# An encoder layer in split fp32: the last pair's operand splits one embedding block later, sums of two output units made in memory, and two gate units' sums one product sooner

## The chip, the cores and the metric

The kernel runs on one core of one Trainium2 chip. The metric is the device time of one execution in microseconds (us). The kernel before takes 2235.86 us (median of 3 runs, 2234.56 to 2236.57).

## What is computed

One layer of a hybrid encoder on 512 tokens of width 2048, in fp32:

```
h   = rms_norm(x);  one projection h @ w_in gives
      group A: banded attention, 16 heads of 64 (own 64-token chunk + 8 before), with a bias
      group B: gated linear attention (GLA), 4 heads, per-head norm, times silu(gate)
x  += concat(group A, group B) @ w_out
x  += conv3-gated FFN of width 5632 (up, gelu, down)
x  += sigmoid(rms_norm(x) @ w_ple_gate) * (p @ w_ple_proj)      p: 512 x 256
out = rms_norm(x)
```

## The kernel before

**Products.** Every large matrix product is cut into *units*: a unit yields a 256-row block of the result in four quarters, and it does so by seven products P1 to P7 instead of eight, as in Winograd's form of Strassen's scheme. The weights' side of the seven is L11, L12, S2, S1, S3, S4 and L22, where S1 = L21+L22, S2 = S1+L11, S3 = L21+L11, S4 = S2+L12; each is a page of 128x1024 (512 KB). The other side is one of seven stored operands, R11, R21, R22, N1, N2, T3, T4, each in two halves of four k-blocks. A product runs in one of three accumulators, accA, accB, accC: P1 and P4 in A, P2 in B, and so on.

**Splits.** TensorE gets its precision from splitting each operand: ScalarE (ACT) writes the rounded high part (`wsplit<-l`, `wsplit<-s`, `wo_R<-...`), VectorE (DVE) subtracts it and writes the low part (`wsplit<-l,wsplit`). A product is 24 matmuls: high by high, high by low, low by high, over 8 k-blocks. An accumulator is collected by ACT if its quarter is new (`u<-accA`) and else added by DVE (`u<-u,accA`).

**Order.** A list `steps` gives one product a step; the first two and the last two units of a stage are interleaved, P1 of both, P2 of both, and so on. `agenda[step]` holds pairs (k, function): k = 0 before the step's weight split, 1 behind its high part, above 1 behind its product. In the main loop ACT, DVE and TensorE (PE) keep this program order (all their rows carry line 64, the helper that does that). The weight split stands two steps ahead of its product.

**Stages.** A value projection; `linear` (GLA heads 16 to 19, values 20 to 23, gate units 8 and 9, in the order 16, 20, 21, 17, 22, 23, 18, 8, 9, 19); `front` (attention units 0 to 7 and gate units 10, 11); then four *embedding blocks* (p @ w_ple_proj, `embedding`, L728), one step each; `wo` (eight units of w_out); the FFN; the last norm. Gate units 8 to 11 are g = 0 to 3. For g below 2, `times` (u = u·on, with `on` the GLA head read back from memory, L860) and `pair` (`store_pair`: three stores of u, four sums `tp` on DVE, four stores, SP's L264) are put behind the unit's products by the list at L872.

**An embedding block** is 24 matmuls of 128x512, `pp<-ps,wsplit`, in four banks of PSUM of its own, that is, four chunks of six. ACT evicts each chunk (`pp_o<-pp`); two chunks make a *pair*, which shares one page and is stored to memory from ACT's own DMA queue (`ppd<-pp_o`, L742). A block has two pairs. The eight pairs use the pages u2, u3, c2, u1, c1, c2, u1, c1, so from the sixth pair on ACT must see a store land before it may evict into the page again: the third block's second pair needs the store of the second block's first pair (c2); the fourth block's two pairs need the stores of the second block's second pair (u1) and of the third block's first pair (c1).

**The operands of wo** are loaded from memory, except the last two k-blocks of each second half (the *tails*): `tails[0]` is the last attention pair (`wo_R<-yp`) and `tails[1]` gate unit 11's u (`wo_R<-u`, sums `wo_N<-tp`, `wo_T<-tp`), which never go to memory. `wo.split(op, 1, False, (1,))` splits such a tail, at the agenda place that the last table of the diff gives. Gate unit 11's u is multiplied by `on` just before.

**Weight sums.** A page of the kind "dma" (`issue`, L390) is loaded with L21 by SP (L409) and L22 or L11 is added to it by an accumulating DMA of GpSimd (POOL, L410); S2 is added up by DVE in a page of its own, and S4 in place of S2 (`s<-s,l`). Wo's first and last two units are of that kind before. A page goes back into `free` when its last use is done, and the next wanted load is issued then.

**Transfers and semaphores.** Plain transfers, of SP and ACT alike, use eight semaphores in rotation, so each also waits for the eighth one before it in the program.

Of the kernel before, what the change touches and what calls it, by code (L numbers as in the profile page):

```python
# [8 lines left out]
F32 = mybir.dt.float32  # L9
# [3 lines left out]
ALU = mybir.AluOpType  # L13
# [30 lines left out]
def encoder_block(ctx: ExitStack, tc: tile.TileContext, A, out):  # L44
# [256 lines left out]

    class Stage:
        def __init__(self, name, units, kb, xd, weights, after, sums, edge, last=PLAIN, begin=None, begin_at=0,
                     chained=False, pace=None, late=(), single=False, groups=None):
            self.name, self.kb, self.xd, self.weights, self.after = name, kb, xd, weights, after
            self.begin, self.begin_at, self.pace, self.late = begin, begin_at, pace, late
            self.chained, self.tail, self.quarter = chained, [None, None], None
            self.n = (4, kb - 4 - 2 * chained)
            self.x = {}
            n = len(units)  # L310
            self.units = [Unit(self, u, last if i >= n - 2 else PLAIN, edge if i < 2 or i >= n - 2 else sums)
                          for i, u in enumerate(units)]
            for i in range(n):
                self.units[i].pos = i
            if single:
                self.groups = [[self.units[i] for i in g] for g in groups or [(i,) for i in range(n)]]
# [13 lines left out]
        def split(self, op, g, body=True, tails=(0, 1)):  # L330
# [6 lines left out]
            if self.chained and g == 1:  # L337
# [4 lines left out]


    NEEDS = {"own": ("L11", "L12", "S1", "S3", "L22"), "dma": ("L11", "L12", "S1", "S2*", "S3", "L22"), "dve": ("L11", "L12", "L21", "L22", "S1*", "S2*"),
             "s3": ("L11", "L12", "L21", "L22", "S1*", "S2*")}

    class Unit:
        def __init__(self, stage, u, order, sums):
            self.stage, self.u, self.order, self.sums = stage, u, order, sums
            self.first, self.head, self.last = False, None, None  # L350
            self.w, self.tag = {}, {}
            self.kind, self.lead = None, self
            if sums in ("own", "dma"):
                self.uses = dict(L11=2, L12=2, S1=2, S2=2, S3=1, L22=1)
                self.made = {"S2", "S4"}
            else:
                self.uses = dict(L11=3, L12=2, S1=2, S2=2, L21=2, L22=2)
                self.made = {"S1", "S2", "S3", "S4"}
            self.parts = dict(C11=2, C12=2, C22=2, C21=1)
            self.have = set()  # L360
            self.left = dict(A=4, B=1, C=2)
            self.o = None
            self.banks = {}

    free, wanted, retired = [], [], []

    def retire(tag):
        if tag in free:
# [21 lines left out]
    def issue():  # L390
        kept, i = 0, 0
        while i < len(wanted):
            unit, name = wanted[i]
            if len(free) <= kept:
                return
            if name[-1] == "*":
                kept += 1
                i += 1
                continue
            wanted.pop(i)  # L400
            n = unit.stage.kb * P
            t = raw_page(unit, name)[:, :n]
            src = lambda q: unit.stage.weights(unit.u, q)
            if name[0] == "L":
                d = nc.sync.dma_start(t, src(name))
                if unit.stage is stages[-1] and unit.last is not None:
                    tc.keep_in_program_order(d)
            else:
                nc.sync.dma_start(t, src("L21"))  # L409
                nc.gpsimd.dma_start(t, src("L22" if name == "S1" else "L11"), accum_op=ALU.add)  # L410
# [41 lines left out]
    def prep_high(i, own=None):  # L452
        if i >= len(steps):
            return None
        unit, prod = steps[i]
        name = PRODUCTS[prod][0]
        n = unit.stage.kb * P
        make(unit, name)
        if prod == unit.order[0] and unit.sums not in ("own", "dma"):
            make(unit, "S1")  # L460
        if i + 1 < len(steps):
            nxt, p = steps[i + 1]
            q = PRODUCTS[p][0]
            if (nxt is unit or nxt.paired) and (q != "S4" or "P6" in nxt.w):
                make(nxt, q)
        if i > 0 and steps[i - 1][1] == "P6" and steps[i - 1][0].paired:
            make(steps[i - 1][0], "S4")
        key = {"S4": "S2"}.get(name, "L21" if name == "S3" and unit.sums not in ("own", "dma") else name)
        raw = unit.w[key]
# [224 lines left out]
    def after_gate(unit):  # L694
# [7 lines left out]

    blk2 = lambda w: lambda m, q: w[m + 8 * (q[1] == "2"), int(q[2]) - 1]
    stages = [Stage("wo", list(range(8)), 8, mixd, blk2(A["w_out"]), after_norm(streams[1], h2d, nffn), "s3", "dma",
                    begin=lambda u: load_x(streams[0], u), begin_at=6, chained=True)]
    order, f0, slots = [], 0, {}
    for ci, n in enumerate(CHUNKS):
        for k in range(n // 2):
# [153 lines left out]
    def after_gates(unit):  # L862
        g, M = unit.u - 8, unit.M

        def times():
            vec.tensor_tensor(unit.o, unit.o, M["on"], ALU.mult)

        def pair():
            ops = store_pair(mixd if g < 3 else None, 3 + g, unit.o[:, 0, :], unit.o[:, 1, :])
            if g == 3:  # L870
                tails[1] = ops

        return [(0, 1, lambda: vec.tensor_tensor(unit.o, unit.o, rb2, ALU.mult)),
                (1 if g < 2 else 0, 1.5, lambda: act.activation(unit.o, unit.o, AF.Silu))] + (
                    [(4, 1, times), (5, 1, pair)] if g < 2 else [(1, 1, times), (1, 3, pair)] if g == 2 else
                    [(0, 3, times), (0, 4, pair)])

    gla = {}
# [262 lines left out]
    for n, p in enumerate(PLAIN):  # L1141
# [4 lines left out]
            agenda[i0 + (15 if kept else n + 5)].append((3, lambda op=op, g=g: wo.split(op, g, True, ())))  # L1146
        at = (7, 7, 8, 9, 15, 10, 11)[n]
        agenda[i0 + at].append((3.5, lambda op=op: wo.split(op, 1, False, (0,))))
        at, k = ((8, 1), (9, 1), (10, 1), (12, 1), (15, 3.6), (14, 3), (15, 3.6))[n]
        agenda[i0 + at].append((k, lambda op=op: wo.split(op, 1, False, (1,))))  # L1150

    def embedding_load(raw):
# [21 lines left out]
    def more_banks():  # L1174
        aux_tags[:] = ["b6", "b7"]
        banks.extend(("b4", "b5"))

    agenda[base[front.units[7]] + 7 + 12].append((5, attention_done))
    agenda[i0 + 11].append((0, more_banks))
# [356 lines left out]
```

## Time and profile before

| | before |
|---|---|
| median of 3 runs | 2235.86 us (2234.56 to 2236.57) |
| the profiled execution's own time | 2234.99 us |
| its span, first to last instruction | 2233.0 us |
| mean granted TensorE clock | 0.997 |
| busy: PE / DVE / ACT / POOL | 2192.7 / 1921.8 / 1339.0 / 158.3 us |
| PE's idle time in the span | 40.3 us |
| chain that ended last: PE / DVE / DMA / ACT | 83% / 8% / 3% / 3% |

All rows below come from the profiled execution. Its time is 1.99 us above its span and 0.87 us below the median. A row of a timeline has the start, the busy time, the engine, the line, the operation, out<-in, the tile, and in brackets the idle time of the engine just before, with what ended it. A "DMA" row of a chain or a bracket is a transfer from issue to landing. One row can stand for several like instructions in succession (x48). The times of places: gate units 8 and 9 end at 300 to 335 us, the embedding blocks run from 597 to 625, and wo's first products from 625 on.

### The profile page before, as it was taken

What the parts mean: (1) busy time and instruction counts of PE and PEld (TensorE: products, weight loads), DVE (VectorE), ACT (ScalarE), POOL (GpSimd) and SP (SyncE); (2) the same over time, 40 slices, a digit from 0 to 9 for tenths busy, and PEclk for the clock granted to TensorE, in tenths of its full rate; (3) what the DMA queues carried; (4) which work ended last, traced back from release to release, by engine and by line L of the source; (5) the groups of instructions that cost most, each with busy time, mean ns of one, the idle gap of its engine ahead of it and who ended that gap; (6) DMA issues with size and microseconds to landing.
All of it is one profiled execution on the core that took longest, in us unless ns stands there. A gap on an engine that the chain in (4) does not pass through costs nothing.

```text
span 2233.0 us, 46278 instructions
## 1 busy us (share of the span) xinstructions
PE 2192.7 (98%) x18588; PEld 2143.9 (96%) x18588; DVE 1921.8 (86%) x2632; ACT 1339.0 (60%) x2005; POOL 158.3 (7%) x196
## 2 busy tenths in 40 slices
PE   9999999999999999999999999999999999999997
PEld 8899999999899989999999999999999999999996
DVE  8476778999879888999888898989898797998988
ACT  9455565777665665555555555555564554666765
POOL 0000000000000100000000000000000100001000
PEclk9999999999999999999999999999999999999998
DMA  7466875667888988888888888888876967879996
GB/s 237 138 183 187 224 204 157 179 187 197 286 253 271 325 237 208 215 230 216 224 218 222 216 224 218 211 223 208 254 235 231 315 231 247 313 252 322 296 288 201
DMA packets 190761, 518.31 MB, mean 232 GB/s; under 512 B 20273, under 2 KB 66609, under 8 KB 190545
## 3 DMA queue, kind: packets, MB, share of 16 engines
q1 hardware_dynamic: 161360, 416.77, 55.0%
q0 software_dynamic: 25920, 93.33, 23.3%
q10 hardware_dynamic: 3264, 5.24, 0.6%
q8 instruction: 146, 2.39, 0.4%
q14 instruction: 71, 0.57, 0.1%
HBM read 441.86 MB, written 71.30 MB: 230 GB/s over the span
## 4 chain that ended last, share of the span: by engine, by line
PE 83%; DVE 8%; DMA 3%; ACT 3%; issue 2%; ACTq 0%; DVEq 0%; SPq 0%; POOL 0%; POOLq 0%
PE accA L64 43%; PE accC L64 22%; PE accB L64 10%; DVE wsplit L64 3%; PE v L244 1%; PE v L243 1%; PE v L242 1%; DMA dn_R<-g_R 1%; PE py L64 1%; PE ptr L64 1%; PE psc L64 1%; DMA ppd<-pp_o 1%; DVE u L64 1%; ACT wsplit L64 1%; DMA dn_N<-g_N 1%
## 5 line engine op out<-in xcount | busy, mean ns | idle before, releaser
L64 DVE TENSOR_TENSOR wsplit<-l,wsplit 128x1024 fp32r<-128x1024 f32 (+1 forms) x478 | 573.2, 1200 | 116.4 <-ACT wsplit L64 115.3
L64 ACT ACTIVATE wsplit<-l 128x1024 fp32r<-128x1024 f32 (+1 forms) x478 | 497.4, 1041 | 283.2 <-PE accC L64 115.3
L64 DVE TENSOR_TENSOR wsplit<-s,wsplit 128x1024 fp32r<-128x1024 f32 (+1 forms) x251 | 300.9, 1200 | 68.0 <-ACT wsplit L64 67.6
L64 ACT ACTIVATE wsplit<-s 128x1024 fp32r<-128x1024 f32 (+1 forms) x251 | 260.5, 1038 | 60.4 <-PE accB L64 36.7
L64 ACT ACTIVATE u<-accA 128x256 f32<-128x256 f32 x302 | 113.9, 377 | 274.1 <-PE accA L64 269.3
L64 PE MATMUL accA<-up_T,wsplit 128*128 128x256 f32 x2112 | 253.5, 276 | 0.4 <-ACT wsplit L64 0.4
L64 PEld LDWEIGHTS accA<-up_T,wsplit 128*128 128x128 f32 x2112 | 245.7, 188 | 0.7 <-ACT wsplit L64 0.6
L64 DVE SCALAR_TENSOR_TENSOR cv<-u,cw,cv 128x511 f32<-128x511 f32 (+1 forms) x176 | 131.5, 747 | 3.1
L410 POOL DMA_DIRECT2D s<-in_w_up x88 | 76.1, 865 | 763.3 <-DMA s<-in_w_up 299.6
L64 PE MATMUL accA<-up_N,wsplit 128*128 128x256 f32 x1056 | 127.1, 276 | 1.3 <-DVE wsplit L64 1.3
L64 PE MATMUL accA<-dn_T,wsplit 128*128 128x256 f32 x1056 | 126.2, 276 | 2.0 <-DVE wsplit L64 1.8
L64 PE MATMUL accC<-up_N,wsplit 128*128 128x256 f32 x1056 | 126.8, 276 | 0.9 <-DVE wsplit L64 0.9
L64 PE MATMUL accB<-up_R,wsplit 128*128 128x256 f32 x1056 | 126.8, 276 | 0.6 <-DVE wsplit L64 0.6
L64 PE MATMUL accA<-up_R,wsplit 128*128 128x256 f32 x1056 | 127.0, 276 | 0.0
L64 PE MATMUL accC<-up_R,wsplit 128*128 128x256 f32 x1056 | 126.5, 276 | 0.0
L64 PEld LDWEIGHTS accA<-dn_T,wsplit 128*128 128x128 f32 x1056 | 122.6, 188 | 2.5 <-DVE wsplit L64 2.1
L64 PEld LDWEIGHTS accA<-up_N,wsplit 128*128 128x128 f32 x1056 | 123.0, 188 | 1.7 <-DVE wsplit L64 1.7
L64 PEld LDWEIGHTS accC<-up_N,wsplit 128*128 128x128 f32 x1056 | 122.9, 188 | 1.1 <-DVE wsplit L64 1.1
L64 PEld LDWEIGHTS accB<-up_R,wsplit 128*128 128x128 f32 x1056 | 122.9, 188 | 0.8 <-DVE wsplit L64 0.8
L64 PEld LDWEIGHTS accA<-up_R,wsplit 128*128 128x128 f32 x1056 | 122.9, 188 | 0.5 <-issue 0.5
L64 PEld LDWEIGHTS accC<-up_R,wsplit 128*128 128x128 f32 x1056 | 122.8, 188 | 0.0
L64 DVE TENSOR_TENSOR l<-l,l 128x1024 f32<-128x1024 f32 (+1 forms) x86 | 102.6, 1193 | 0.0
(337 smaller groups left out, 4207.3 us busy)
## 6 DMA issues: line engine op xcount, KB each, us to landing
l<-in_w_up SPq DMA_DIRECT2D x132, 512.0 KB, 4.5
s<-in_w_up SPq DMA_DIRECT2D x88, 512.0 KB, 4.9
s<-in_w_up POOLq DMA_DIRECT2D x88, 512.0 KB, 6.2
l<-in_w_dn SPq DMA_DIRECT2D x56, 448.0 KB, 5.3
l<-in_w_blk SPq DMA_DIRECT2D x48, 512.0 KB, 4.9
s<-in_w_blk SPq DMA_DIRECT2D x32, 512.0 KB, 4.3
s<-in_w_blk POOLq DMA_DIRECT2D x32, 512.0 KB, 7.8
l<-in_w_out SPq DMA_DIRECT2D x28, 512.0 KB, 5.0
```

The costliest lines, as they stand in the source:

```text
L64: ins = f(*args, **kw)
L242: nc.tensor.matmul(ps[t], x[:, 0, sl], wh, start=kt == 0, stop=False)
L243: nc.tensor.matmul(ps[t], x[:, 0, sl], wl, start=False, stop=False)
L244: nc.tensor.matmul(ps[t], x[:, 1, sl], wh, start=False, stop=kt == KD - 1)
L410: nc.gpsimd.dma_start(t, src("L22" if name == "S1" else "L11"), accum_op=ALU.add)
```

## The change

**One, embedding blocks.** For R11, R21 and N2 the split of gate unit 11's tail moves one step, which is one embedding block, later: from (8,1), (9,1), (10,1) to (9,1), (10,1), (11,1).

**Two, sums in memory.** Wo's first two units become of a new kind "mem": seven pages, L11, L12, S2, S1, S3, S4, L22, each used once and each a plain load by SP. `memory_sums` makes the four sums in DRAM ahead of that, by eight transfers for each unit: SP copies w_out's L21 to S1 and to S3, then S1 to S2 and S2 to S4; POOL adds L22 to S1, L11 to S2 and S3, L12 to S4. Order shows a copy as 512x256, rows of 1 KB, and a page load as 128x1024, rows of 4 KB. The sixteen stand on the agenda at steps 12, 18, ..., 102, ahead of each step's weight split; unit 0's at 12 to 54, unit 1's at 60 to 102. In return four accumulates of POOL into pages and four sums of DVE (128x1024) go away, and SP's page loads for the two units become 14 instead of 10. In the whole program DVE has 4 instructions fewer, POOL has 4 DMAs more, SP 12 more; PE and ACT have the same number.

**Three, gate units.** For gate units 8 and 9 `times` and `pair` move one product sooner, from (4,1), (5,1) to (3,1), (4,1).

```diff
-            self.units = [Unit(self, u, last if i >= n - 2 else PLAIN, edge if i < 2 or i >= n - 2 else sums)
+            self.units = [Unit(self, u, last if i >= n - 2 else PLAIN, head if i < 2 else edge if i >= n - 2 else sums)
...
+             "mem": ("L11", "L12", "S2", "S1", "S3", "S4", "L22"),
...
+    def memory_sums(unit):
+        n = unit.stage.kb * P
+        w = lambda q: unit.stage.weights(unit.u, q)
+        for q in ("S1", "S2", "S3", "S4"):
+            in_memory[unit, q] = dp.tile([P, n], F32, name=f"{unit.stage.name}{unit.u}{q}")
+        S = lambda q: in_memory[unit, q]
+
+        def first(q, src):
+            tc.keep_in_program_order(nc.sync.dma_start(S(q), src, max_dma_last_dim=n))
+
+        def added(q, src):
+            tc.keep_in_program_order(nc.gpsimd.dma_start(S(q), src, accum_op=ALU.add, max_dma_last_dim=n))
+
+        return [lambda: first("S1", w("L21")), lambda: added("S1", w("L22")), lambda: first("S3", w("L21")),
+                lambda: first("S2", S("S1")), lambda: added("S2", w("L11")), lambda: added("S3", w("L11")),
+                lambda: first("S4", S("S2")), lambda: added("S4", w("L12"))]
...
-            if name[0] == "L":
+            if name[0] == "L" or unit.sums == "mem":
+                src = src if name[0] == "L" else lambda q: in_memory[unit, q]
                 d = nc.sync.dma_start(t, src(name))
...
-                    begin=lambda u: load_x(streams[0], u), begin_at=6, chained=True)]
+                    begin=lambda u: load_x(streams[0], u), begin_at=6, chained=True, head="mem")]
...
-                    [(4, 1, times), (5, 1, pair)] if g < 2 else [(1, 1, times), (1, 3, pair)] if g == 2 else
+                    [(3, 1, times), (4, 1, pair)] if g < 2 else [(1, 1, times), (1, 3, pair)] if g == 2 else
...
-        at, k = ((8, 1), (9, 1), (10, 1), (12, 1), (15, 3.6), (14, 3), (15, 3.6))[n]
+        at, k = ((9, 1), (10, 1), (11, 1), (12, 1), (15, 3.6), (14, 3), (15, 3.6))[n]
         agenda[i0 + at].append((k, lambda op=op: wo.split(op, 1, False, (1,))))
...
+    for n, op in enumerate(op for u in wo.units[:2] for op in memory_sums(u)):
+        agenda[12 + 6 * n].append((0, op))
```

**Where instructions stand.** The first place is ACT's order between the first and the second embedding block's evictions; the rows below are of before, `wsplit<-l` is a weight split and `pp_o<-pp` the second block's first pair.

```order
L64 ACTIVATE wo_R_6943<-yp 128x256
L64 ACTIVATE wo_R_7007<-yp 128x256
L64 ACTIVATE wsplit<-l_6966 128x1024
L64 ACTIVATE wo_R_6943<-u 128x256
L64 ACTIVATE pp_o<-pp 128x512 x2
L742 DMA ppd<-pp_o 128x2x512
```

The split of gate unit 11's u stands ahead of the pair. After the change the same place on ACT reads so:

```order
L64 ACTIVATE wo_R_6967<-yp 128x256
L64 ACTIVATE wo_R_7031<-yp 128x256
L64 ACTIVATE wsplit<-l_6990 128x1024
L64 ACTIVATE pp_o<-pp 128x512 x2
L767 DMA ppd<-pp_o 128x2x512
```

The pair follows the weight split directly. The rows of ACT after the second block's second pair, up to the third block's first pair, are now these:

```order
L64 ACTIVATE wo_N_7077<-wo_N_7077 128x1024
L64 ACTIVATE wo_N_7110<-wo_N_7110 128x512
L64 ACTIVATE wo_N_7075<-tp 128x256
L64 ACTIVATE wsplit<-l_7041 128x1024
L64 ACTIVATE wo_R_6967<-u 128x256
L64 ACTIVATE pp_o<-pp 128x512 x2
```

The split that was moved, R11's, stands here now, where R21's stood before; R21's and N2's moved likewise by a block each.

The second place is DVE's order around gate unit 9's sums, while GLA unit 19's products run; before it is this, with `u<-u,on` for `times`, `tp` for the four sums of `pair`, and `u<-u,accA` for the collection of unit 19's accumulator.

```order
L64 TENSOR_TENSOR dd<-cs 128x512
L64 TENSOR_TENSOR wsplit<-l_2964,wsplit 128x1024
L64 TENSOR_TENSOR u<-u,on 128x1024
L64 TENSOR_TENSOR wsplit<-l_3199,wsplit 128x1024
L64 TENSOR_TENSOR u<-u,accA 128x256
L64 TENSOR_TENSOR tp<-u 128x256 x2
L64 SCALAR_TENSOR_TENSOR tp<-tp,u 128x256 x2
L64 TENSOR_TENSOR wsplit<-l_3229,wsplit 128x1024
```

The collection stands ahead of the four `tp` sums. After the change DVE has this there:

```order
L64 TENSOR_TENSOR dd<-cs 128x512
L64 TENSOR_TENSOR u<-u,on 128x1024
L64 TENSOR_TENSOR wsplit<-l_2979,wsplit 128x1024
L64 TENSOR_TENSOR tp<-u 128x256 x2
L64 SCALAR_TENSOR_TENSOR tp<-tp,u 128x256 x2
L64 TENSOR_TENSOR wsplit<-l_3215,wsplit 128x1024
L64 TENSOR_TENSOR u<-u,accA 128x256
L64 TENSOR_TENSOR wsplit<-l_3246,wsplit 128x1024
```

The four sums and a weight split stand ahead of the collection now. The third place is SP's order at gate unit 8's stores (`mix_R<-u`), where `l` is a page load; before:

```order
L405 DMA l_3199<-in_w_blk 128x1024
L405 DMA l_3229<-in_w_blk 128x1024
L405 DMA l_3262<-in_w_blk 128x1024
L264 DMA mix_R_116<-u 128x256
L264 DMA mix_R_118<-u 128x256
L264 DMA mix_R_120<-u 128x256
```

Three page loads stand ahead of the three stores of u. After the change one of the three is a copy in memory:

```order
L429 DMA l_3215<-in_w_blk 128x1024
L429 DMA l_3246<-in_w_blk 128x1024
L381 DMA wo1S_213<-in_w_out 512x256
L264 DMA mix_R_116<-u 128x256
L264 DMA mix_R_118<-u 128x256
L264 DMA mix_R_120<-u 128x256
```

Unit 1's first copy (S1 from L21) took the place of a page load, which comes behind unit 8's stores now.

More of the change, by code (lines that the diff above doesn't have):

```diff
@@ L303, in __init__ @@
         def __init__(self, name, units, kb, xd, weights, after, sums, edge, last=PLAIN, begin=None, begin_at=0,
-                     chained=False, pace=None, late=(), single=False, groups=None):
+                     chained=False, pace=None, late=(), single=False, groups=None, head=None):
+            head = head or edge
             self.name, self.kb, self.xd, self.weights, self.after = name, kb, xd, weights, after
@@ L352, in __init__ @@
             self.kind, self.lead = None, self
-            if sums in ("own", "dma"):
+            if sums == "mem":
+                self.uses = {name: 1 for name in NEEDS["mem"]}
+                self.made = set()
+            elif sums in ("own", "dma"):
                 self.uses = dict(L11=2, L12=2, S1=2, S2=2, S3=1, L22=1)
@@ L365, in encoder_block @@
     free, wanted, retired = [], [], []
+    in_memory = {}
+    def memory_sums(unit):
[11 more added lines that the diff above has]
+                lambda: first("S4", S("S2")), lambda: added("S4", w("L12"))]
     def retire(tag):
@@ L458, in prep_high @@
         make(unit, name)
-        if prod == unit.order[0] and unit.sums not in ("own", "dma"):
+        if prod == unit.order[0] and unit.sums not in ("own", "dma", "mem"):
             make(unit, "S1")
@@ L468, in prep_high @@
         key = {"S4": "S2"}.get(name, "L21" if name == "S3" and unit.sums not in ("own", "dma") else name)
+        key = name if unit.sums == "mem" else key
         raw = unit.w[key]
```

## The prediction

> **What bounds the kernel now.** I read the page first, then the PE, ACT and DVE timelines at the two places that the change touches, then the chain of waits there, then the busy windows. On the page I look at the share of PE and at what the chain that ended last is made of.
>
> ```profile
> span 2233.0 us, 46278 instructions
> PE 2192.7 (98%) x18588; PEld 2143.9 (96%) x18588; DVE 1921.8 (86%) x2632; ACT 1339.0 (60%) x2005; POOL 158.3 (7%) x196
> q1 hardware_dynamic: 161360, 416.77, 55.0%
> q0 software_dynamic: 25920, 93.33, 23.3%
> PE 83%; DVE 8%; DMA 3%; ACT 3%; issue 2%; ACTq 0%; DVEq 0%; SPq 0%; POOL 0%; POOLq 0%
> L64 ACT ACTIVATE wsplit<-s 128x1024 fp32r<-128x1024 f32 (+1 forms) x251 | 260.5, 1038 | 60.4 <-PE accB L64 36.7
> ```
>
> PE is idle for 2233.0 − 2192.7 = 40.3 us. PE's count doesn't change, so the change can win only PE waits, or stretched matmuls. The last row says that ACT's splits of sum pages wait for PE, not for a page to arrive. The PE timeline around the embedding blocks has the largest wait near the change:
>
> ```profile
> 597.22 11.07 PE L64 MATMUL pp<-ps,wsplit 128*128 128x512 f32 x48
> 612.36 12.77 PE L64 MATMUL pp<-ps,wsplit 128*128 128x512 f32 x48 [4.08 <-ACT pp_o L64]
> 624.97 5.62 PE L64 MATMUL accA<-wo_R,wsplit 128*128 128x256 f32 x48
> 631.28 5.08 PE L64 MATMUL accB<-wo_R,wsplit 128*128 128x256 f32 x40 [0.70 <-ACT wsplit L64]
> 637.52 1.18 PE L64 MATMUL accB<-wo_R,wsplit 128*128 128x256 f32 x8 [1.15 <-DVE wsplit L64]
> ```
>
> The first row is blocks one and two, the second three and four, then P1 and P2 of wo's first pair of units. Within reach: 4.08, then 12.77 − 11.07 = 1.70 that the second row holds inside, 0.70 and 1.15. ACT's timeline shows what they wait for (an eviction x2 is a pair, ppd the store of a pair):
>
> ```profile
> 603.52 0.37 ACTq L742 DMA_DIRECT2D ppd<-pp_o  x1
> ...
> 608.25 1.04 ACT L64 ACTIVATE wsplit<-l 128x1024 fp32r<-128x1024 f32 x1
> 611.41 0.42 ACT L64 ACTIVATE wo_R<-u 128x256 fp32r<-128x256 f32 x1 [2.11 <-DVE u L64]
> 611.73 1.07 ACT L64 ACTIVATE pp_o<-pp 128x512 f32<-128x512 f32 x2
> 613.17 0.37 ACTq L742 DMA_DIRECT2D ppd<-pp_o  x1
> ...
> 618.15 1.06 ACT L64 ACTIVATE pp_o<-pp 128x512 f32<-128x512 f32 x2
> 619.25 0.37 ACTq L742 DMA_DIRECT2D ppd<-pp_o  x1
> 621.25 1.09 ACT L64 ACTIVATE pp_o<-pp 128x512 f32<-128x512 f32 x2 [2.04 <-DMA ppd<-pp_o]
> ...
> 626.87 1.09 ACT L64 ACTIVATE pp_o<-pp 128x512 f32<-128x512 f32 x2 [0.50 <-ACT pp_o L64]
> 630.19 1.04 ACT L64 ACTIVATE wsplit<-l 128x1024 fp32r<-128x1024 f32 x1
> 633.18 1.05 ACT L64 ACTIVATE wsplit<-l 128x1024 fp32r<-128x1024 f32 x1
> ```
>
> ACT stood 2.11 us for gate unit 11's u, which DVE was multiplying, with the second block's evictions behind it, and PE's third block needs a bank from those. Later it stood 2.04 for a store to land. The DVE rows and the transfers of the chain of waits:
>
> ```profile
> 610.15 1.23 DVE L64 TENSOR_TENSOR u<-u,on 128x1024 f32<-128x1024 f32 x1 [1.07 <-DMA on<-ond]
> ...
> 634.78 1.21 DVE L64 TENSOR_TENSOR s<-s,l 128x1024 f32<-128x1024 f32 x1
> ...
> 636.25 1.22 DVE L64 TENSOR_TENSOR wsplit<-l,wsplit 128x1024 fp32r<-128x1024 f32 x1
> ```
> ```profile
> 603.52 9.57 DMA ppd<-pp_o
> ...
> 613.17 8.00 DMA ppd<-pp_o
> ```
> ```profile
> DMA to landing us min/median/max: 4.9/8.3/10.9
> ```
>
> The last row is that of the tile ppd, over its eight stores.
>
> **Part one, tails a block later.** The pair of 611.73 comes right behind the split of 608.25, which hands over to the next instruction at about 609.2. PE's third block can start 612.36 − 611.73 = 0.63 after it, at 609.85: 2.5 us sooner. The price is that the third block's first pair still stands behind a split of that u, but u is ready at 611.4, and ACT gets there at 609.2 + (618.15 − 611.73) − 0.3 = 615.3, so that split waits for nothing. The pair's store (page c2) issues at about 610.3. The third block's second pair needs its landing: with 4.9 us, the quickest, at 615.2, with the 8.00 of now at 618.3, with 10.9 at 621.2. I take 617, since four of POOL's accumulates leave those microseconds (part two). So that pair runs at 617.0 instead of 621.25. PE's fourth block has its last two chunks (half of 5.5) behind it: from 618.6, after its first two, which start at 615.9, to 621.4. Before it ended at 624.97, so PE gains 3.6 here, 0.6 if the store takes the longest.
>
> Then P1 of both units (5.6 us, covered by operands split long before) runs to 627.0. P2 needs L12, whose split is 630.19 − 626.87 = 3.32 behind the start of the fourth block's second pair. That pair takes the page of the third block's first pair (store of 619.25 now, issued at about 616.4 then), and with 8 us of transfer it starts at 624.4 (622.3 with the quickest value plus an eviction's wait, 627.3 with the longest). The split ends at 628.7: PE waits 1.7 there and starts P2 2.6 sooner than at 631.28. Of the 3.6, 1.0 is lost to this store.
>
> The moved instructions have no DMA of their own. DVE's low parts of the same tails move along (0.4 us each) behind the weight split of their step, and PE reads them in P1 at the earliest. One queue moves: SP's loads of R22's second half and T4 now share semaphores with ACT's first two stores, so T4 and what SP has behind it (loads of S1 and S3) issue when the second store lands, 603.52 + 9.57 = 613.1. T4's split stands behind L12's of 630.19, 17 us on, where the longest landing of the row above is 10.9: covered, and S1 and S3 are used later still. If it weren't, P2's second unit would wait behind T4 on ACT.
>
> **Part two, sums in memory.** Gone at wo's start is DVE's S2 sum of 634.78, which stood ahead of the second L12's low part (636.25), for which PE waits 1.15. Without it P2's second unit doesn't stop: the second high part is ready 633.18 − 630.19 = 3.0 behind the first, 0.3 more for a moved tail split between them, at 632.1; with half of 5.6 the pair ends at 634.9, where it ended at 637.52 + 1.18 = 638.7. So at the end of P2 the gain is 3.8, of which 1.2 is this part's. The other three sums go from a DVE that PE doesn't wait for there: 0.
>
> The price lies from 100 to 480 us, and the windows show what room there is (the last two columns are the DMA share and GB/s):
>
> ```profile
> 100.00:480.00 380.00, 376.03 (x3188) 360.86 (x3187) 295.58 (x481) 230.30 (x372) 27.58 (x33) 1.00 0.68 186
> 300.00:315.00 15.00, 15.00 (x124) 14.00 (x123) 10.26 (x14) 5.50 (x8) 0.86 (x1) 1.00 1.01 291
> 600.00:640.00 40.00, 34.07 (x194) 29.42 (x193) 28.96 (x39) 28.25 (x47) 3.45 (x4) 0.96 0.98 318
> ```
>
> No row shows a copy from memory to memory. By q1's row, 0.55 × 2233 us for 416.77 MB, 512 KB (0.524 MB) takes 1.54 us of all 16 engines; by q0's row, accumulates, 2.92. Eight of each are 8 × 4.46 = 36 us of engine time in a stretch with 0.32 × 380 = 122 us free. As the row of ACT's sum splits shows pages ahead of their use, I take 0 there, with 1.5 us as the other bound for pages that come late in a full patch. Near wo four accumulates become plain loads, 4 × (2.92 − 1.54) = 5.5 us less for engines that are 0.98 busy, which is why I put the ppd stores below 8 us. The Trainium skill, page "DMA: Bandwidth & Descriptors", section "Issuing engines are not separate DMA queues", speaks against this part: whoever issues a transfer, it runs on the same 16 engines, so moving sums from DVE to POOL's queue buys nothing while they are full. The trace agrees in the window of 300 to 315, at a share of 1.01; where it is 0.68 no run here decides it.
>
> **Part three, gate units.** PE's rows behind unit 8's and unit 9's sums, and what ACT and DVE did:
>
> ```profile
> 321.11 3.00 PE L64 MATMUL accA<-in_T,wsplit 128*128 128x256 f32 x24 [1.86 <-ACT u L64]
> ...
> 327.38 2.98 PE L64 MATMUL accA<-in_T,wsplit 128*128 128x256 f32 x24 [0.55 <-ACT wsplit L64]
> ...
> 336.33 0.46 PE L64 MATMUL pat<-eb,en 128*128 128x128 f32 x2 [0.53 <-DVE eb L64]
> ```
> ```profile
> 313.09 0.38 ACT L64 ACTIVATE u<-accA 128x256 f32<-128x256 f32 x1 [4.80 <-DMA mix_R<-u]
> ```
> ```profile
> 326.82 0.41 DVE L64 TENSOR_TENSOR u<-u,accA 128x256 f32<-128x256 f32 x1
> 327.15 0.75 DVE L64 TENSOR_TENSOR tp<-u 128x256 f32<-128x256 f32 x2
> 327.82 0.87 DVE L64 SCALAR_TENSOR_TENSOR tp<-tp,u 128x256 f32<-128x256 f32 x2
> ```
> ```profile
> 303.54 9.45 DMA mix_R<-u
> ```
>
> ACT waits 4.80 until unit 8's u is stored and its page free, and from that backlog PE loses 1.86. The stores would come a product (2.7 us) sooner. But they land when the engines have worked off what is queued ahead, at a share of 1.01, and that is as much as before: unit 1's first copy stands in the place of one page load, 512 KB for 512 KB. I take +0.2 (bounds −1.9, the stall gone, and +1.4, the copy at an accumulate's 2.92).
>
> For unit 9 DVE's four tp sums (0.75 + 0.87, about 1.5) now stand ahead of the collection of 326.82, which empties the accumulator for PE's product of 327.38: that start goes to about 328.9, +1.5. PE's wait of 0.53 at 336.33 is for DVE's eb, which has the same work ahead of it as before, so that wait shrinks, and its backlog takes back a bit more: I keep +0.7 (bounds 0 and +1.5).
>
> **Sum.** −3.8 (embedding to P2) + 0.2 + 0.7 + 0 = −2.9, against the profiled execution 2234.99 − 2.9 = 2232.1. The median stands 0.87 above it, so I forecast 2235.86 − 2.9 = 2233.0. The bounds of the embedding part are −5.8 (both stores quick) and −0.5 (both slow). The measurement can tell about 0.2%, which is 4.5 us here.
>
> **Rivals.**
>
> A, the forecast: 2233.0, its own range 2231.2 to 2235.2. Chance 0.52.
>
> B, stores land early at both places: unit 8's page is free before ACT asks, so −1.9 instead of +0.2, and the embedding part is at −4.4; with unit 9's +0.7 that is −5.6, 2230.3. For it: the stores are 128 KB each, and the stretch after 315 isn't full on average. Against: 1.01. The Trainium skill, page "DMA: Bandwidth & Descriptors", section "Queues, rings and completion order", has each engine take turns between the queue rows that have work, so with POOL's row empty near 610 the ppd stores would get a larger share; that leans to B's side at the embedding, and no run here shows it yet. Chance 0.24.
>
> C, the embedding's gain is given back: the third and fourth blocks' second pairs wait for their stores as now, 8 to 10.9 us, since SP's fourteen page loads fill what the accumulates leave. Then PE ends blocks and P2 only 0.6 sooner, and part three costs its 0.9: +0.3, 2236.2, no change that can be told. For it: the chain row of 9.57 and the share of 0.98. Chance 0.15.
>
> D, slower: a copy between memory rows is priced by packet, not by byte. A 512 KB page load is 128 rows of 4 KB, 8 for each engine; the copy is 512 rows of 1 KB, 32 for each. At an accumulate's 2.92 / 8 = 0.365 us a packet one copy is 11.7 us of all engines. It stands right ahead of unit 8's stores, so ACT's page comes 11.7 − 1.5 = 10 us later, and PE, which runs one accumulator ahead, stops for it. With the −2.9 otherwise the result is +7.1: 2243.0. It is slower than before from a copy of 1.5 + 2.9 = 4.4 us on, by over 0.2% from 8.9. Against: plain loads move a packet far quicker (0.55 × 2233 × 16 / 161360 = 0.12 us). Chance 0.09.
>
> **Numbers.** Faster by over 0.2% (under 2231.4): B but for its upper edge, 0.20, and A's lower edge, 0.08: 0.28. Slower: D, 0.09. Within: 0.63. The range 2229.7 to 2236.8 leaves out D and B's far end.
>
> **What would show it.** Right: PE's 4.08 ahead of the third block shrinks to about 1.6, the two blocks' row to about 11.5, the 1.15 for DVE's wsplit at P2 is gone, ACT's split of u no longer waits, its wait for mix_R stays near 4.8 and PE's product of 327.38 starts about 1.5 later against its forerunners. Wrong: a wait of over 3 us for ppd at the fourth block (C), ACT's wait for mix_R under 3 (B) or over 8, with a copy of over 4 us landing just before it (D), or sum pages that ACT waits for between 100 and 480.

## The result, and the profile after

The changed kernel takes 2244.19 us (median of 6 runs, 2241.54 to 2248.46) against 2235.62 (6 runs, 2234.56 to 2236.57): a ratio of 1.0035, 95% interval 1.0025 to 1.0045. It is slower by 8.6 us. Its profiled execution took 2243.28 us, 8.29 above that of before.

On the page after, look at PE and at the two DMA queues:

```profile
span 2241.3 us, 46302 instructions
...
PE 2197.7 (98%) x18588; PEld 2147.9 (96%) x18588; DVE 1918.6 (86%) x2628; ACT 1339.9 (60%) x2005; POOL 163.7 (7%) x200
...
q1 hardware_dynamic: 166160, 423.06, 55.9%
q0 software_dynamic: 29568, 95.43, 24.1%
```

PE's idle time grew from 40.3 to 2241.3 − 2197.7 = 43.6 us, only 3.3 of the 8.3. PE's *busy* time grew by 5.0 for the same 18588 matmuls, so some of them ran slower. Since PE's order is the same in both, the start of one matmul after minus its start before is the time lost up to there, its *drift*. The PE timeline of before, in a stretch that the prediction never looked at:

```profile
262.85 2.88 PE L64 MATMUL accB<-in_R,wsplit 128*128 128x256 f32 x24
...
268.17 3.03 PE L64 MATMUL accA<-in_N,wsplit 128*128 128x256 f32 x24
...
271.39 3.00 PE L64 MATMUL accC<-in_N,wsplit 128*128 128x256 f32 x24
```

and the same work after:

```profile
263.70 1.98 PE L64 MATMUL accB<-in_R,wsplit 128*128 128x256 f32 x16
268.15 2.08 PE L64 MATMUL accB<-in_R,wsplit 128*128 128x256 f32 x8 [2.47 <-DVE wsplit L64]
271.90 0.77 PE L64 MATMUL pat<-eb,en 128*128 128x128 f32 x2 [1.68 <-DVE eb L64]
...
276.41 3.95 PE L64 MATMUL accA<-in_N,wsplit 128*128 128x256 f32 x24
...
280.55 3.00 PE L64 MATMUL accC<-in_N,wsplit 128*128 128x256 f32 x24
```

PE is 0.85 us late at 263.70 and 9.16 late at 280.55: 8.3 us are lost here, as much as the whole result. The two waits make 4.15 of it. The rest is in the lengths: 24 matmuls of `accA<-in_N` take 3.95 instead of 3.03. The windows show why, in the third column from the end, the granted clock; after:

```profile
260.00:270.00 10.00, 7.53 (x59) 7.26 (x57) 4.34 (x6) 2.66 (x4) 0.00 (x0) 0.91 0.80 190
270.00:280.00 10.00, 8.32 (x41) 6.76 (x40) 6.22 (x9) 1.06 (x1) 1.05 (x2) 0.58 0.56 173
```

and before:

```profile
270.00:280.00 10.00, 10.00 (x85) 9.84 (x84) 5.25 (x8) 4.20 (x6) 1.72 (x2) 1.00 1.02 263
```

0.58 where before had 1.00, and 41 matmuls in the 10 us instead of 85. Elsewhere the gains and losses nearly cancel. The embedding blocks and wo's start are where the prediction had its gain; the rows to compare are those from 597.22 to 637.52:

```profile
609.88 11.07 PE L64 MATMUL pp<-ps,wsplit 128*128 128x512 f32 x48
622.49 5.74 PE L64 MATMUL pp<-ps,wsplit 128*128 128x512 f32 x24 [1.54 <-ACT pp_o L64]
...
634.14 5.62 PE L64 MATMUL accA<-wo_R,wsplit 128*128 128x256 f32 x48
640.92 3.09 PE L64 MATMUL accB<-wo_R,wsplit 128*128 128x256 f32 x24 [1.16 <-ACT wsplit L64]
644.22 3.33 PE L64 MATMUL accB<-wo_R,wsplit 128*128 128x256 f32 x24 [0.21 <-ACT wsplit L64]
647.38 2.88 PE L64 MATMUL accA<-wo_N,wsplit 128*128 128x256 f32 x24
```

From the first block to the end of P2, where the products of `wo_N` begin, it is 647.38 − 609.88 = 37.50 us. Before, these products begin here:

```profile
638.54 5.60 PE L64 MATMUL accA<-wo_N,wsplit 128*128 128x256 f32 x48
```

So it was 638.54 − 597.22 = 41.32. The gain is 3.8 us, the prediction's number. The wait of 4.08 is 1.54 and the 1.15 for DVE's wsplit is gone.

At the gate units:

```profile
330.60 3.03 PE L64 MATMUL accA<-in_T,wsplit 128*128 128x256 f32 x24 [1.87 <-ACT u L64]
...
338.34 4.17 PE L64 MATMUL accA<-in_T,wsplit 128*128 128x256 f32 x24 [1.84 <-DVE u L64]
```

The stall of 1.86 stayed at 1.87, and the product of 327.38 came 338.34 − 327.38 = 10.96 late where its forerunner at 321.11 was 330.60 − 321.11 = 9.49 late: +1.5 for the four sums ahead of the collection, as worked out. The 24 matmuls there then take 4.17 for 2.98. From 280 us to the first embedding block the kernel loses 609.88 − 597.22 = 12.66 less 9.16, 3.5 us, of which the prediction had 0.9.

What did PE wait for near 265? DVE's timeline after, at the sum S2 of a GLA unit, which adds a sum page `s` to a page `l`:

```profile
265.66 1.22 DVE L64 TENSOR_TENSOR l<-l,s 128x1024 f32<-128x1024 f32 x1 [5.67 <-DMA s<-in_w_blk]
```

Before, the same sum didn't wait:

```profile
259.05 1.22 DVE L64 TENSOR_TENSOR l<-l,s 128x1024 f32<-128x1024 f32 x1
```

The page came late: the chain of waits after has its load by SP and its accumulate by POOL.

```profile
251.31 5.42 DMA s<-in_w_blk
...
257.28 8.28 DMA s<-in_w_blk
```

Before, the two took 4.5 and 7.1 us, so 2.1 us of the delay are in their lengths. The larger part is the *issue*: 251.31 where before had 245.37, which is 5.1 us beyond PE's drift of 0.86 there. SP's own waits, from 225 to 260 us, say why (line waited for: us in total, times, longest):

```profile
SPq L885 <- DMA vad<-vo: 13.1, 2, 12.2
```

The same view of before has

```profile
SPq L860 <- DMA vad<-vo: 6.4, 1, 6.4
```

That line (885 after, 860 before) loads `on` for gate unit 8. It needs a page out of which value unit 23 is still being stored (`vad<-vo`). SP issues in order, so everything behind it waits too, the next sum pages first. The two stores that stand ahead of that line took twice as long; the tile vad, whose first two stores are alone in the window, from 230 to 250 us after:

```profile
DMA to landing us min/median/max: 13.1/13.4/13.6
```

and from 230 to 240 us before:

```profile
DMA to landing us min/median/max: 6.6/6.8/6.9
```

What shared the engines with them is the new work; the issues of after, from 225 to 270 us, with the median from issue to landing last:

```profile
wo0S<-in_w_out POOLq DMA_DIRECT2D x2, 512.0 KB, 15.6
```

These are wo unit 0's accumulates into S2 and S3. That gave the theory, called S below: **two accumulates in memory slow the value stores, the stores hold the load of `on`, that load holds SP's queue, the queue delays a sum page that had little slack, and PE stops.** Its rivals: that the sums cost by their 1 KB rows (theory P, near the prediction's D), or by their number in the queues whatever their rows (Q); that part three is to blame (G); and that the engines' time is simply short, whoever issues in what order (E). The first four runs set P, G and Q against each other; S and E were told apart after them.

### The profile page after: what moved, and what is told of

It is laid out like the page before. It is cut to its first block, busy times and chain, and to the rows that moved or that the text cites. A ratio compares the mean times of both kernels' runs of the same rounds, so it can differ in the third digit from the quotient of the medians.

```text
span 2241.3 us, 46302 instructions
## 1 busy us (share of the span) xinstructions
PE 2197.7 (98%) x18588; PEld 2147.9 (96%) x18588; DVE 1918.6 (86%) x2628; ACT 1339.9 (60%) x2005; POOL 163.7 (7%) x200
## 3 DMA queue, kind: packets, MB, share of 16 engines
q1 hardware_dynamic: 166160, 423.06, 55.9%
## 4 chain that ended last, share of the span: by engine, by line
PE 77%; DVE 10%; DMA 8%; issue 2%; ACT 2%; SPq 0%; DVEq 0%; ACTq 0%; POOLq 0%
PE accA L64 39%; PE accC L64 20%; PE accB L64 10%; DVE wsplit L64 4%; DMA s<-in_w_blk 1%; PE v L242 1%; PE v L243 1%; PE v L244 1%; DMA s<-in_w_v_a 1%; DVE l L64 1%; DVE u L64 1%; PE py L64 1%; DMA dn_R<-g_R 1%; DMA s<-in_w_dn 1%; ACT wsplit L64 1%
```

## The experiments

Each was run beside the kernel before on the same chip, and each ratio is against those runs.

**One part at a time.** The first three kernels are before with one part of the change each. The edit of the first is the last table of the diff alone:

```diff
-((8, 1), (9, 1), (10, 1), (12, 1), ...
+((9, 1), (10, 1), (11, 1), (12, 1), ...
```

> Part one alone on the kernel before (tails of R11, R21, N2 one embedding block later). The trace of the whole change shows the drift between the kernels fall from 13.1 to 8.8 us between 612 and 638 us, 4.2 us, of which the missing S2 sum was put at 1.2. Both theories below expect -2 to -4 us here (0.9982 to 0.9991), with the wait of 4.08 for pp_o at 1.5 to 2, and no difference before 600 us. If it is within 0.5 us of before, the gain came from the sums in memory and not from the moved tails.

2234.13 us against 2236.20, ratio 0.9990 (0.9981 to 0.9999). Part one alone is a gain of 2 us. Its PE timeline:

```profile
596.47 11.07 PE L64 MATMUL pp<-ps,wsplit 128*128 128x512 f32 x48
609.07 5.74 PE L64 MATMUL pp<-ps,wsplit 128*128 128x512 f32 x24 [1.54 <-ACT pp_o L64]
...
635.18 1.18 PE L64 MATMUL accB<-wo_R,wsplit 128*128 128x256 f32 x8 [1.16 <-DVE wsplit L64]
636.20 5.60 PE L64 MATMUL accA<-wo_N,wsplit 128*128 128x256 f32 x48
```

636.20 − 596.47 = 39.73 us up to the first product of `wo_N`, 1.6 less than before, with the wait for DVE still there.

The second has the kind "mem" and its transfers, with the tables of parts one and three as before.

> Part two alone on the kernel before (sums of wo's first two units in memory, rows of 1 KB). Theory P (the copies and accumulates between rows of memory cost by packet, 512 each, and hold up SP's queue and the page loads around 230 to 265 us): +6 to +11 us, with a stop of PE of over 2 us near 265 us and a lower granted clock behind it. Theory G (the two gate units' sums are what costs, the memory sums are hidden): -1 to 0 us.

2244.45 us, ratio 1.0040 (1.0028 to 1.0053): part two alone costs as much as the whole change. So it is theory P's side, not G's. At 270.48 and at 274.24 us its PE has stopped for 2.58 us each time, as it did near 265 in the whole change, and the granted clock is 0.64 from 270 to 280 us. Its PE timeline at wo's start:

```profile
611.66 11.07 PE L64 MATMUL pp<-ps,wsplit 128*128 128x512 f32 x48
627.03 12.79 PE L64 MATMUL pp<-ps,wsplit 128*128 128x512 f32 x48 [4.30 <-ACT pp_o L64]
639.65 5.62 PE L64 MATMUL accA<-wo_R,wsplit 128*128 128x256 f32 x48
645.11 5.60 PE L64 MATMUL accB<-wo_R,wsplit 128*128 128x256 f32 x48
650.55 5.60 PE L64 MATMUL accA<-wo_N,wsplit 128*128 128x256 f32 x48
```

650.55 − 611.66 = 38.89 us, 2.4 less than before, although the wait of 4 us is there: P1 and P2 run without a stop. The benefit of part two is real and twice what I gave it; it is paid for 350 us earlier.

The third moves `times` and `pair` only: `[(4, 1, times), (5, 1, pair)]` to `[(3, 1, times), (4, 1, pair)]`.

> Part three alone on the kernel before (gate units 8 and 9 a product sooner). The prediction's own term is +0.7 for unit 9 and -1.9 to +0.2 for unit 8. Theory P: -1.2 to +1.5 us, with PE's product that began at 327.38 us late by about 1.5 against its forerunners and no stop near 265 us. Theory G: +5 us or more.

2236.30 us, ratio 1.0001 (0.9992 to 1.0010): no difference that can be told. In its trace PE doesn't stop near 265 us, and the product of 327.38 comes 1.5 late against its forerunner, both as expected. But the stall at unit 8 shrinks from 1.86 to 0.61: without a copy ahead of them the earlier stores do land sooner.

**Rows of 4 KB.** The fourth is the whole change with larger rows: `max_dma_last_dim` counts bytes here, so `n` = 1024 gave rows of 256 elements.

```diff
-nc.sync.dma_start(S(q), src, max_dma_last_dim=n)
+nc.sync.dma_start(S(q), src, max_dma_last_dim=4 * n)
...
-nc.gpsimd.dma_start(S(q), src, accum_op=ALU.add, max_dma_last_dim=n)
+nc.gpsimd.dma_start(S(q), src, accum_op=ALU.add, max_dma_last_dim=4 * n)
```

> The whole change, but the sums in memory are copied and accumulated in rows of 4 KB, 128 for each transfer instead of 512 of 1 KB; the bytes, the places and the order are the same. Theory P: a copy takes about 4 to 6 us from issue to landing instead of 5 to 13, an accumulate 6 to 9 instead of 10 to 17, the stop near 265 us goes or falls under 1 us, and the time is 2230 to 2236, that is 8 us or more below the whole change. Theory Q (what counts is that sixteen transfers more stand in the queues of SP and POOL, ahead of page loads, whatever their rows): still +6 to +9 against before.

2243.46 us, ratio 1.0038 (1.0025 to 1.0050): as slow. Its issues between 225 and 270 us, and DVE's sum:

```profile
wo0S<-in_w_out POOLq DMA_DIRECT2D x2, 512.0 KB, 12.4
```
```profile
265.68 1.23 DVE L64 TENSOR_TENSOR l<-l,s 128x1024 f32<-128x1024 f32 x1 [6.13 <-DMA s<-in_w_blk]
```

With a quarter of the packets the two accumulates are 3 us quicker, 12.4 for 15.6, not down to the 6 to 9 that P expected, and that helps nothing: the value stores still land after 12.6 us in the median, since the two are in flight beside them all the same. Theory P, and with it the price by packets of rival D, falls as the cause. Theory Q's expectation held, but whether by the order or by the engines' time wasn't told apart yet.

**The queue or the engines.** The fifth leaves all sixteen transfers where they are and takes only the blocked instruction out of the way: the load of `on` stands behind the next loads on SP. (It isn't needed soon: in the whole change it is issued at 249.84 and its product runs at 307.61.)

```diff
-        nc.sync.dma_start(unit.M["on"], ond[g])
+        d = nc.sync.dma_start(unit.M["on"], ond[g])
+        if g == 0:
+            tc.keep_in_program_order(d)
...
-                agenda[base[u] + (3, 6, 3, 6)[u.u - 8]].append(...
+                agenda[base[u] + (4, 6, 3, 6)[u.u - 8]].append(...
```

> The whole change, with gate unit 8's load of on (64 KB... 512 KB, from ond) put behind the next unit's page loads on SP's queue, where it stood ahead of them; nothing else moves. Theory S (unit 23's value stores, slowed from 6.6 to 13.1 us by two accumulates in memory, hold up the load of on, which waits for their page, and SP's whole queue behind it, so that the next sum pages come 6 us late): the wait of DVE for the s page falls from 5.67 to under 1.5 us, PE's drift at 269 us from 8.9 to under 3, the time is 2235 to 2239. Rival E (the accumulates take the 16 engines' time, and the page loads come late whoever issues when): DVE's wait stays above 4 us, the time 2241 to 2247.

2233.87 us (12 runs), ratio 0.9995 (0.9981 to 1.0008): the time of before again, by one load's place, where the whole change had a ratio of 1.0035. The median lies 1.1 us below S's range. Two of the twelve runs, 2242.67 and 2247.06, were as slow as the whole change; what happened in them no trace shows. The tile vad of this kernel, from 230 to 252 us, DVE's sum and the window:

```profile
DMA to landing us min/median/max: 9.3/11.3/13.7
```
```profile
261.60 1.22 DVE L64 TENSOR_TENSOR l<-l,s 128x1024 f32<-128x1024 f32 x1
```
```profile
260.00:270.00 10.00, 10.00 (x86) 9.48 (x84) 9.84 (x13) 4.89 (x7) 0.00 (x0) 1.00 0.70 206
```

The stores are as slow as without the edit, up to 13.7 us, but the sum page is there when DVE asks, PE doesn't stop there and the clock stays at 1.00. That is theory S against E. PE's drift is 2.56 here, within S's 3, and all of it was lost at one wait near 200 us (last section).

**Another place, two fewer.** The sixth puts the sixteen at `agenda[70 + 4 * n]`, among the attention units; the seventh leaves out the transfers numbered 4 and 5, the two accumulates.

> The whole change, with the sixteen transfers of the sums put on steps 70, 74, ..., 130 instead of 12, 18, ..., 102, that is into the attention units (about 340 to 580 us) and away from the stretch up to 265 us. Theory S: no stop near 265, and since attention's pages have no such load in SP's queue ahead of them, 2231 to 2236. Rival E: their 36 us of engine time cost as much wherever they stand, 5 us or more of PE waits appear between 340 and 600 us, the time is 2240 to 2246.

> The whole change without two of its sixteen transfers: wo unit 0's S2 doesn't get L11 added and its S3 doesn't get L11 added, so that unit's S2, S3 and S4 leave L11 out. These are the two accumulates in flight from 227 to 249 us. If those two cause the stop (theories S and E alike): 2234 to 2238, no stop near 265. If it is the copies, or the sum of all sixteen: 2240 or more.

The sixth takes 2235.97 us (12 runs), ratio 1.0000 (0.9990 to 1.0010), and has no wait of PE near 265. It lies at the edge of S's range: the stop is avoided, but the gain at wo's start doesn't show in the time. In its trace PE is 5.1 us behind before when the embedding starts and wins 3.4 of them back by the end of P2, and 2.7 of the 5.1 were lost among the attention units, so there the transfers aren't free either. The seventh takes 2234.87 (12 runs), ratio 0.9992 (0.9983 to 1.0002): without the two the 8 us are gone, with fourteen transfers in place. DVE's sum:

```profile
264.95 1.22 DVE L64 TENSOR_TENSOR l<-l,s 128x1024 f32<-128x1024 f32 x1
```

It doesn't wait. (Its profiled execution, 2239.39 us, is the slowest of the twelve; it lost 4.2 us near 200, see the last section.)

**Both edits.** The eighth has the fourth's rows and the fifth's place.

> Both edits: the load of on behind the page loads, and the sums in rows of 4 KB. Theory S: as the first of these, and up to 2 us less: 2233 to 2238. Rival E: 2240 or more, since the rows alone gave 0.7 us.

2235.55 us (12 runs), ratio 0.9996 (0.9985 to 1.0006): inside S's range; the rows add nothing to the place.

**The two alone.** The run that settles the cause is before with four unused transfers:

```diff
+    more = [dp.tile([P, 1024], F32, name=f"more{i}") for i in range(2)]
+    wl = lambda q: blk2(A["w_out"])(0, q)
...
+    for i in range(2):
+        agenda[(12, 24)[i]].append((0, lambda i=i: more_first(i)))
+        agenda[(36, 42)[i]].append((0, lambda i=i: more_added(i)))
```

> The kernel before with four transfers more whose result nobody uses: two copies of w_out blocks in memory at steps 12 and 24, two accumulates of 512 KB onto them at steps 36 and 42, where the whole change has wo unit 0's S2 and S3. Nothing else is changed. Theory S: the two accumulates are enough for the stop: DVE waits 4 to 7 us for the s page near 260, PE's drift there is 6 to 9 us, and the time is 2242 to 2246. If it takes all sixteen, or the changed order of wo's loads: 2235 to 2238.

2245.92 us, ratio 1.0044 (1.0030 to 1.0057): two copies and two accumulates of 512 KB, which nobody reads, cost this kernel 10 us, and in its trace 10.2 us are lost at the stop. The copies had landed at 188.0, long before it. Its DVE row and its waits of SP are those of the whole change:

```profile
266.51 1.23 DVE L64 TENSOR_TENSOR l<-l,s 128x1024 f32<-128x1024 f32 x1 [6.09 <-DMA s<-in_w_blk]
```
```profile
SPq L860 <- DMA vad<-vo: 13.1, 1, 13.1
```

Together with the seventh, which has the copies and not the two accumulates: the two are enough, and without them there is no stop.

**Looking for a better version.** Three kernels use what was learned. The first has parts one and two, the load of `on` moved, and the sums at `agenda[38 + 6 * n]`; the second is before with the moved load alone; the third is part one with the moved load.

> Parts one and two with two edits, and without part three: gate unit 8's load of on stands behind the page loads on SP's queue, and the sixteen transfers on steps 38, 44, ..., 128. Theory S: no stop near 198 (no copy is in flight there any more, which made DVE's wait for a sum page 1.4 us), none near 265, and 4 us gained at wo's start: 2230 to 2234, below before by 2 to 6. Rival E (engine time costs wherever it is spent): 2236 to 2242.

> The kernel before with one edit, gate unit 8's load of on behind the page loads. Theory S: before has SP's queue held for only 7 us there and its sum page lands 1.5 us ahead of DVE's use, so nothing is to be won: 2235 to 2237, within 1 us of before. If the queue's hold costs before too: 2232 to 2234.

> Part one alone, with the load of on behind the page loads: sums on DVE and POOL as before. Theory S: as part one alone, 2233 to 2235; the later load adds nothing without the accumulates in memory.

The first takes 2234.43 us, ratio 0.9993 (0.9985 to 1.0002): above S's range and not the 2 to 6 us hoped for. Its PE and ACT timelines show a new stop:

```profile
316.70 3.02 PE L64 MATMUL accA<-in_N,wsplit 128*128 128x256 f32 x24 [2.94 <-ACT u L64]
```
```profile
316.26 0.38 ACT L64 ACTIVATE u<-accA 128x256 f32<-128x256 f32 x1 [7.78 <-DMA mix_R<-u]
```

The S2 accumulate is now in flight while gate unit 8's stores run, ACT waits 7.78 us for them instead of 4.80, and PE's drift goes from 0.1 to 4.3 us between 300 and 400 us, as much as it wins at wo's start, 4.2. It is rival D's place, through an accumulate beside the stores. The second takes 2234.91, ratio 0.9996 (0.9987 to 1.0004), within 1 us of before as S expected: without the accumulates the queue's hold of 6.4 us costs nothing. The third takes 2233.61, ratio 0.9990 (0.9982 to 0.9999), which is part one alone again. So the best version found is part one alone, by 2 us, and nothing that keeps part two beats it.

## Why the prediction was wrong

**Embedding and wo's start, −3.8: right**, 41.32 − 37.50 = 3.8 measured. The pieces were not: I gave part one 2.6 and part two 1.2; alone, each in one profiled execution, they make 1.6 and 2.4. The third block started 1.54 after the wait began, as 1.6 was forecast, and the fourth block's second pair waited 1.87 for its store. One reading behind the number was wrong. I took the 1.70 us that the row of the third and fourth block held inside for a wait, and gave blocks three and four a gain of 1.1 by earlier stores. But PE didn't wait inside that row of before; the clock was halved behind the wait of 4.08:

```profile
613.60:617.00 3.40, 3.40 (x9) 2.67 (x8) 2.18 (x3) 2.96 (x6) 0.00 (x0) 0.50 1.05 261
```

After the change the two blocks took 634.14 − 622.49 = 11.65 us instead of 12.61 because the clock stayed up, which I hadn't forecast: this piece of the 3.8 came out by luck.

**Unit 9, +1.5 at its product: right**, 10.96 − 9.49 = 1.5. **Unit 8, stall stays: right**, 1.87, and for the reason given: with part three alone, where no copy stands ahead of the stores, it fell to 0.61. What followed from them to the embedding was 3.5 in the profiled execution and 0.9 in the sum. Of the 3.5, 1.2 is the product at 338.34, whose matmuls took 4.17 instead of 2.98 at a granted clock of 0.84 (340 to 350 us); how much of the rest belongs to the waits of part two's other transfers in that stretch is open. Alone, part three is at 1.0001.

**The failed step is the price of part two, "I take 0 there, with 1.5 us as the other bound for pages that come late in a full patch."** What the step had wrong is where a late page is waited for and how late a page may be: it measured 8.3 us at one place. Three errors made it.

The first is the row that I took for cover. I read "ACT's splits of sum pages wait for PE, not for a page" as "pages are ahead of their use". But a sum page S1 has an earlier user, DVE's `l<-l,s`. Before's own DVE timeline showed it, had I asked for it:

```profile
194.96 1.23 DVE L64 TENSOR_TENSOR l<-l,s 128x1024 f32<-128x1024 f32 x1 [0.21 <-DMA s<-in_w_v_a]
```

That is another GLA unit's and value unit's stretch, 64 us ahead of the stop, and DVE already waits 0.21 us for a page there: no slack at all. At the sum of the stop the slack was 1.5 us. Before, the page's accumulate was issued at 250.40, with this time to landing, and DVE's sum began at 259.05:

```profile
DMA to landing us min/median/max: 7.1/7.1/7.1
```

After, it landed at 257.28 + 8.28 = 265.56, which is 7.2 us later than before if the drift of 0.86 is taken off; less the 1.5 that is the wait of 5.67. The sign of being wrong that I named, sum pages that ACT waits for between 100 and 480, didn't show, since it was DVE that waited.

The second is the mean. 36 us of engine time against 122 us free is about right as a sum and says nothing about two accumulates that fall on the stores for which SP's queue stands. Two at my 2.92 make 5.8 us; they measured 3.4 each (last section), 6.7 together, and the two stores took 13.1 and 13.6 where they took 6.6 and 6.9. So the price per transfer was near enough; the place of payment was not looked for. Going through SP's waits in before (6.4 us on `vad<-vo`) would have found the one line where a delay passes on to everybody. The Trainium skill, page "DMA: Bandwidth & Descriptors", section "Issuing engines are not separate DMA queues", which I cited against this part, is borne out: transfers of POOL's queue slowed SP's stores from 6.9 at most to 13.6. I had weighed it by the mean share of 0.68 only.

The third is the clock. I counted waits as waits. Here 4.15 us of waiting cost 8.3, the rest by a granted clock of 0.58 from 270 to 280 us.

**Rival D** gave 2243.0, and 2244.19 was measured, but by another way. A 1 KB row copy does take long (11.16 us for the one that stands ahead of unit 8's stores), yet against before PE lost nothing by it there: 1.87 against 1.86.

```profile
310.36 11.16 DMA wo1S<-in_w_out
```

What the copy took was a gain of part three, with which alone that stall fell to 0.61. Nor does a packet have one price: a 1 KB packet of an accumulate took 105 ns, a 4 KB one 364 (last section). D's number was met by chance. The chance of 0.09 for slower was too low because I had only one mechanism for it.

## What to carry to other kernels

When transfers are added to a kernel whose PE hardly waits, don't price them by the mean share of the DMA engines. List the instructions on which an in-order queue stands for a landing, and for each page that is loaded there its *first* user and how long it lands before it; a delay is free only up to the smallest of these. An instruction that is needed late but stands early in such a queue is worth moving before anything is added.

## What the runs showed of the hardware

**A short stop of PE can cost more than itself.** In the kernel without the two accumulates the windows show it by itself, after one wait of 1.29 us at 200.53:

```profile
200.53 0.46 PE L64 MATMUL pat<-eb,en 128*128 128x128 f32 x2 [1.29 <-DVE eb L64]
```
```profile
200.00:210.00 10.00, 9.47 (x49) 8.47 (x50) 5.68 (x7) 1.73 (x3) 0.00 (x0) 0.66 0.36 91
```

The clock was 0.66 over the window, with 49 matmuls where before has 82, and the drift grew by 4.2 us. With the load of `on` moved, a like wait of 1.30 us at that place was followed by less:

```profile
200.00:210.00 10.00, 10.00 (x67) 9.35 (x66) 6.42 (x9) 2.29 (x3) 0.88 (x1) 0.83 0.27 62
```

There the drift grew by 2.7 us, wait and all. In these traces the granted clock was either whole or halved, and the halved stretch behind the wait lasted 3.41 us in that kernel, 6.83 without the two accumulates and 10.24 behind the stop of the whole change. Not every wait is followed by one: in the whole change the wait of 1.87 at 330.60 was not (its 24 matmuls took 3.03 us), the one of 1.84 at 338.34 was. The Trainium skill, page "TensorE: Matmul & The Clock Gate", section "HAM oscillation — how this bites in real kernels", puts the limit at idle gaps of about 3.4 us; here a gap of 1.29 and a pair of 2.47 and 1.68 were followed by a lowered clock, so the measurement decides: a gap below that limit can cost clock too.

**The engines' time went by bytes more than by rows.** The packets in the traces give it directly. The eight accumulates in memory of the whole change are 4096 packets of 1 KB on POOL's queue, 105 ns each in the mean; shared out over 16 engines that is 3.4 us for one accumulate. In the fourth run all of POOL's packets are 4 KB, and they took 364 ns, 2.9 us for 512 KB. The eight copies in rows of 1 KB added 13.5 us of 16 engines to the packets of that size on SP's and ACT's queue, 1.7 each; packets of 4 KB there took 193 ns, 1.5 us for 512 KB. (The shares on the pages can't tell such differences: with the same transfers q1 has 55.9% of the span in the whole change and 55.4% with part two alone.) This fits the value stores: two accumulates make 6.7 us in rows of 1 KB and 5.8 in rows of 4 KB, and the first two stores took 6.5 and 6.7 us longer with the one and 5.8 with the other.

What stays open: the kernels of the fifth to eighth run scatter more than before does beside them (2233.0 to 2240.5). The one with the moved load ran from 2229.69 to 2247.06 us over 12 runs, and only its profiled execution shows what was waited for.
